# Windowed attention of a hybrid backbone: one pass over the scores, with the exponentials transposed on TensorE

## The chip, the cores and the metric

The kernel runs on one core of one Trainium2 chip. The metric is the device time of one execution in microseconds (us). A core has a matrix engine (TensorE, PE in the profile, with its weight loads as PEld), a vector engine (VectorE, DVE), an activation engine (ScalarE, ACT), a general engine (GpSimd, POOL) and a queue for transfers (SyncE, SP). Each runs its own instructions in a fixed order and waits for the others by semaphores.

## What is computed

Two layers of a transformer-like backbone over 256 context tokens and 1024 latent tokens of width 1024. In each layer one input projection feeds three mixers, whose outputs are concatenated and go through one output projection; a gated MLP follows. The change concerns the third mixer, attention in a window, with 8 query heads of width 64 in two groups of four that share keys and values:

```
s_loc = einsum(q, kw) * scale          # keys of the query's block of 128 and of both neighbours
s_loc = where(|kpos - qpos| <= 128, s_loc, NEG_INF)
s_ctx = einsum(q, kc) * scale          # all 256 context keys
p = softmax(concat([sink, s_ctx, s_loc], -1))
o = p[ctx] @ vc + p[loc] @ vw
```

Context queries attend to the 256 context keys alone, and only in layer 0. Everything is float32; the kernel reaches that precision on TensorE by splitting values into a high and a low part of type fp32r and adding the products.

## The kernel before

Tokens are in 10 blocks of 128, blocks 0 and 1 being context. `gq_units` (L1446) makes one unit for each block of queries and each group of heads: 20 units in layer 0 (4 of them context, with 2 blocks of keys) and 16 in layer 1. A latent unit has 5 blocks of keys, 2 of context and 3 local ones, or 4 at the ends of the sequence; the two layers have 84 and 76 pairs of unit and key block. A unit has two parts, each a generator.

`scores` (L1477) only finds row maxima. Queries are on the partitions of the output: for each of four heads a product of the high parts over 128 rows (L1498) and one of the leftovers over 64 rows (L1499), over 256 context columns and over up to 384 local ones, each into a bank of PSUM named `gs`. VectorE reduces them (L1505 for context, L1512 for local, which also adds the band mask), takes the minimum with the sink (L1516, L1518), and `max_rows` (L1214) turns the four columns of maxima into rows of the query tile by a product with the identity (L1223, into `mT`).

`values` (L1522) computes the scores again, this time with keys on partitions and the four heads' queries in 512 columns, with the maxima now subtracted by the product itself: for each block of keys a mask product where needed (L1544), the high product (L1546) and the leftovers and maxima (L1547), into a `gs` bank. ScalarE takes the exponential into `gx` (L1550), VectorE rounds it to `gp`'s high part (L241), GpSimd subtracts for the low part (L245), and three products with V follow (L1555 to L1557, into `o`), delayed by up to four blocks (`GDL`). V has a column of ones, so that row 64 of `o` is the sum of the exponentials. `unflip` (L1228) copies `o` and transposes it back (L1235, into `yT`).

What sets the order: `streams` walks over the units' two parts by their costs, with up to `GQL` units of lead for `scores`, and a scheduler then places each engine's instructions, the unit before (`df_units`, the second mixer) having the higher priority (`HPO`). So the windowed attention begins while the second mixer ends. In that mixer, score products over 512 columns go to `ds` (L1376, L1363), ScalarE takes exponentials in place (L1356), later products go to `ds` again (L1419), ScalarE takes exponentials (L1420) and the product with V is L1432; L1412 transposes its result by a product with `fold`.

The banks are what the two share least: `df_p` holds three (two `ds`, one `od`), and the windowed attention has these:

```
p_b = self.psum(f"pb{l}", {n: ("b", 4) for n in (None, "gs", "mT", "yT")})
p_o = self.psum(f"po{l}", {"o": ("o", 1)} if ODB + XB == 3 else {})
```

So `gs`, `mT` and `yT` take turns in four banks, and the result has one. The band mask `band3` has a place of its own in both layers. The output projection of the first blocks (L249 to L251, into `op`; its transposes L1630) is already woven into the end of the windowed attention.

## Time and profile before

| | us |
|---|---|
| median of 3 runs | 4549.56 |
| lowest and highest | 4540.59, 4586.83 |
| the profiled execution | 4560.47 |
| span of the profiled execution | 4558.6 |
| PE busy | 4169.8 (91%) |
| PEld busy | 3182.7 (70%) |
| DVE busy | 2917.1 (64%) |
| ACT busy | 1797.8 (39%) |
| POOL busy | 2180.7 (48%) |

The span runs from the first to the last instruction. Matmuls are pipelined, so that the record of one begins before that of the one ahead has ended: what a product costs in a stream is the distance from its start to the next start, not its length. A product of plain float32 data has two records. The granted clock of TensorE has two levels, 2.4 GHz (1.00 in the views) and 1.2 GHz (0.50), and a stretch's figure is the mean; over the span it is 0.892.

### The profile page before, as it was taken

The numbers are of one execution on the slowest core, as the hardware profiler recorded it, in microseconds if no ns is written. First come the engines' busy times: TensorE is split into PE (matmuls) and PEld (weight loads), VectorE is DVE, ScalarE is ACT, GpSimd is POOL, SyncE is SP. The second block draws the span as 40 slices with busy tenths as digits, with TensorE's granted clock in tenths as the row PEclk, the third lists the DMA queues.
The fourth block names the chain that finished last, engine by engine and source line by source line (L and its number), as shares of the span: only waits on it lengthen the run. The fifth ranks groups of instructions, "written<-read, shape, count | busy, mean of one in ns | idle before, by whom it ended". The sixth has DMA issues, their size and how long they took to land.

```text
span 4558.6 us, 67583 instructions
## 1 busy us (share of the span) xinstructions
PE 4169.8 (91%) x24447; PEld 3182.7 (70%) x24447; DVE 2917.1 (64%) x5849; ACT 1797.8 (39%) x3586; POOL 2180.7 (48%) x2151
## 2 busy tenths in 40 slices
PE   8998888898998799979998998888989998999898
PEld 5886655665466699968996786645845466788786
DVE  4346676567665877788777336766677656766443
ACT  3334554544323333343333334555534333333332
POOL 3335324334353666666665425264243445766443
PEclk9997778796899899989998998668988988999999
DMA  6454232234023222232223646132241142222443
GB/s 205 137 135 109 62 85 78 69 95 119 27 68 126 93 84 78 81 116 88 79 84 114 166 115 144 43 80 60 59 121 34 29 133 87 79 83 84 146 149 121
DMA packets 465626, 440.44 MB, mean 97 GB/s; under 512 B 122115, under 2 KB 389515, under 8 KB 465292
## 3 DMA queue, kind: packets, MB, share of 16 engines
q1 hardware_dynamic: 408780, 369.39, 27.4%
q0 software_dynamic: 24352, 62.80, 4.9%
q10 hardware_dynamic: 32160, 3.94, 0.5%
q8 instruction: 193, 3.16, 0.3%
q14 instruction: 141, 1.16, 0.1%
HBM read 340.96 MB, written 95.04 MB: 96 GB/s over the span
## 4 chain that ended last, share of the span: by engine, by line
PE 73%; DVE 13%; DMA 5%; ACT 3%; issue 3%; POOL 2%; SPq 1%; ACTq 0%; DVEq 0%; POOLq 0%
PE m L249 6%; PE m L250 6%; PE m L251 6%; PE b L249 3%; PE b L250 3%; PE od L1432 3%; PE b L251 3%; PE gs L1499 2%; PE gram L955 2%; PE dn L249 2%; PE dn L250 2%; PE dn L251 2%; PE ds L1419 2%; PE gs L1498 2%; PE fm L249 2%
## 5 line engine op out<-in xcount | busy, mean ns | idle before, releaser
L245 POOL TENSOR_TENSOR gp<-gx,gp 128x512 fp32r<-128x512 f32 x160 | 208.4, 1307 | 257.3 <-DVE gp L241 181.9
L239 ACT ACTIVATE fwh<-wraw 128x1024 fp32r<-128x1024 f32 x198 | 206.0, 1055 | 273.0 <-DVE wraw L1849 190.8
L1356 ACT ACTIVATE ds<-ds,dnm 128x512 f32<-128x512 f32 (+1 forms) x400 | 232.4, 581 | 189.2 <-DVE dnm L1378 112.4
L1420 ACT ACTIVATE p<-ds 128x512 f32<-128x512 f32 (+1 forms) x336 | 187.2, 585 | 254.8 <-PE ds L1419 211.8
L245 DVE TENSOR_TENSOR wl<-wraw,fwh 128x1024 fp32r<-128x1024 f32 x110 | 196.8, 1790 | 114.0 <-ACT fwh L239 111.8
L245 POOL TENSOR_TENSOR wl<-wraw,fwh 128x1024 fp32r<-128x1024 f32 x88 | 222.4, 2530 | 95.8 <-ACT fwh L239 95.5
L249 PE MATMUL m<-h,fwh 128*128 128x322 f32 (+1 forms) x660 | 219.8, 333 | 11.0 <-ACT fu L1895 6.8
L1378 DVE TENSOR_REDUCE dnm<-ds 128x1 f32<-128x512 f32 x256 | 173.6, 686 | 84.9 <-PE ds L1376 82.2
L251 PE MATMUL m<-h,wl 128*128 128x322 f32 (+1 forms) x660 | 218.8, 332 | 2.9 <-DVE wl L245 2.9
L245 DVE TENSOR_TENSOR wl<-wr,wh 128x512 fp32r<-128x512 f32 (+1 forms) x76 | 66.6, 878 | 241.8 <-ACT wh L239 128.2
L250 PE MATMUL m<-h,fwh 128*128 128x322 f32 (+1 forms) x660 | 220.1, 334 | 0.0
L245 POOL TENSOR_TENSOR wl<-wr,wh 128x512 fp32r<-128x512 f32 (+1 forms) x76 | 99.8, 1313 | 246.8 <-ACT wh L239 208.1
L1425 DVE SCALAR_TENSOR_TENSOR p<-p,ls 128x512 f32<-128x512 f32 (+1 forms) x168 | 144.8, 863 | 95.3 <-ACT p L1420 93.3
L1432 PE MATMUL od<-p,vh 128*64 128x512 f32 (+1 forms) x336 | 191.0, 707 | 13.4 <-DVE p L1425 9.2
L1376 PE MATMUL ds<-ks,qs 96*128 96x512 f32 x256 | 155.5, 625 | 44.5 <-ACT ds L1356 37.5
L250 PE MATMUL dn<-dl,ahl 128*128 128x512 f32 x440 | 177.5, 403 | 4.4 <-POOL dl L245 4.4
L249 PE MATMUL dn<-dh,ahl 128*128 128x512 f32 x440 | 175.3, 402 | 5.2 <-ACT ahl L239 3.8
L245 POOL TENSOR_TENSOR dl<-dr,dh 128x1024 fp32r<-128x1024 f32 x44 | 109.5, 2489 | 143.2 <-ACT dh L239 143.2
L249 PE MATMUL m<-T,fwh 128*128 128x322 f32 (+1 forms) x436 | 147.1, 338 | 32.7 <-DVE fraw L1866 23.7
L251 PE MATMUL dn<-dh,ahl 128*128 128x512 f32 x440 | 171.4, 399 | 0.0
L1419 PE MATMUL ds<-qs,ks 104*128 104x512 f32 (+1 forms) x336 | 152.7, 496 | 8.8 <-ACT p L1420 5.9
L245 DVE TENSOR_TENSOR dd<-dr,dd 128x1024 fp32r<-128x1024 f32 x44 | 59.0, 1344 | 156.9 <-ACT dd L239 156.9
(572 smaller groups left out, 13490.3 us busy)
## 6 DMA issues: line engine op xcount, KB each, us to landing
dr<-in_ff_w_down_dram SPq DMA_DIRECT2D x88, 512.0 KB
aw<-in_ada_w_dram SPq DMA_DIRECT2D x160, 256.0 KB
wraw<-in_ff_w_gate_dram SPq DMA_DIRECT2D x66, 512.0 KB
wraw<-in_ff_w_up_dram SPq DMA_DIRECT2D x66, 512.0 KB
wr<-in_w_in_dram SPq DMA_DIRECT2D x88, 256.0 KB
x<-scr_x SPq DMA_DIRECT2D x28, 512.0 KB
scr_act<-cv POOLq DMA_DIRECT2D x22, 512.0 KB, 3.0
ar<-scr_act SPq DMA_DIRECT2D x44, 256.0 KB
```

Of the source, the lines that this page charges most:

```text
L239: nc.scalar.activation(hi, src, AF.Copy)
L245: e.tensor_tensor(out=lo, in0=src, in1=hi, op=ALU.subtract)
L249: mm(out, lh, rh, start=first, stop=False)
L250: mm(out, lh, rl, start=False, stop=False)
L251: mm(out, ll, rh, start=False, stop=last)
L1356: act.activation(s, s, AF.Exp, bias=nm[:, c, m, i:i + 1], accum_out=L[:, c, m, i:i + 1])
L1376: mm(s, us["q"][m][0:96, i * 128:i * 128 + 128], K2[m][0:96, 256 + 512 * c:768 + 512 * c], start=True, stop=True)
L1378: vv.tensor_reduce(out=nm[:, 1 + c, m, i:i + 1], in_=s, axis=AX.X, op=ALU.max, negate=True)
L1419: mm(s[:, :w], hs["K"][m][0:104, j * 128:j * 128 + 128], us["q"][m][0:104, :w], start=True, stop=True)
L1420: act.activation(p[:, m, :w], s[:, :w], AF.Exp)
L1425: vv.scalar_tensor_tensor(out=p[:, 0, :w], in0=p[:, 1, :w], scalar=self.nlam, in1=p[:, 0, :w], op0=ALU.mult, op1=ALU.add)
L1432: mm(o[r:r + 64, :w], v[:, j], p[:, 0, :w], start=j < 2, stop=j >= nk - 2)
```

## The change

Each unit now makes one pass. `scores` takes the heads in pairs, (0, 2) and (1, 3). A pair's local scores go to two `gs` banks and its context scores to a third. VectorE finds the maxima as before, and ScalarE then takes the exponentials from the same banks, with queries on partitions, the maximum as a bias and the sum as an accumulated output (L1542, L1544 of the new kernel), into a tile `ge` for each head. `max_rows`, the mask product and the column of ones are gone. `values` transposes the exponentials, four heads to a `gs` bank (L1571), ScalarE copies the bank to the high part (L1573), VectorE subtracts for the low part from PSUM (L1574), and two products follow: the high part with [V high, V low] side by side in 128 columns (L1580), and the low part with V high (L1581). The result's two halves are added by a float32 product with `gfold` (L1563). The leftovers of heads 2 and 3 lie on partitions 64 to 127 of the query and key tiles, so that a pair's leftover products use different row halves (L1508; the high products are L1504). Leads and delays become 1, `gp` has three buffers, and a unit's second pair is not begun before the unit ahead has issued its transposes. The costs that `streams` uses change. In layer 0 `band3` takes a buffer of the tag `cv`, and it is loaded by SP's queue where it was GpSimd's.

```diff
-GQL = (2, 2)
+GQL = (1, 1)
...
-GPB = 4
+GPB = 3
...
-GXB = 2
-GDL = (4, 4)
-GHI = "v"
-GLO = "p"
+GDL = (1, 1)
...
     def gq_consts(self):
-        self.mask8 = self.mask("mask8", 64)
-        self.identr = self.al("identr", [128, 128], 1, F32R)
-        self.nc.vector.tensor_copy(self.identr, self.ident)
+        self.gfold = self.al("gfold", [128, 64])
+        for i in range(2):
+            self.nc.gpsimd.tensor_copy(self.gfold[64 * i:64 * i + 64], self.ident[64 * i:64 * i + 64, 64 * i:64 * i + 64])
         self.band3 = None
...
+                            self.cast(k[0:64], self.scr_gk[g, 128:192, tok])
+                            self.cast(k[64:128], self.scr_gk[g, 128:192, tok])
...
+                v = [self.al(t, [128, n, 128], b, F32R, "gv") for t, n, b in (("hA0", 5, 8), ("fB", 4, 8), ("gv", 1, 2))]
...
-            us = {}
+            us = {"before": prev[0]}
+            prev[0] = us
...
-                    self.band3 = self.al("band3", [128, 384], 1, F32R)
-                    self.cast(self.band3, self.a["k_band"])
+                    self.band3 = self.al("band3", [128, 384]) if l == DEPTH - 1 else self.al("cv", [128, 384], 2, n="band3")
+                    self.load(self.band3, self.a["k_band"])
...
+                self.cast(q2[64:128, 256:512].rearrange("p (h t) -> p h t", h=2), src[0:64, 2:4])
...
+                for hp in ((0, 2), (1, 3)):
+                    if hp[0] and us["before"]:
+                        while not us["before"].get("done"):
+                            yield 0.3
+                    n2 = slice(hp[0], 4, 2)
+                    sl = []
+                    if nloc:
+                        sl = [self.bk("gs") for _ in hp]
+                        for k, c, x in pieces(kts[2], nloc):
+                            for s, h in zip(sl, hp):
+                                main(s[:, x], h, k, c)
+                            for s, h in zip(sl, hp):
+                                rest(s[:, x], h, k, c, h // 2)
                         b = (kts[2] - qt + 1) * 128
...
+                        for s, h in zip(sl, hp):
+                            vv.tensor_tensor_reduce(out=s[:, :nloc * 128], in0=s[:, :nloc * 128], in1=self.band3[:, b:b + nloc * 128],
+                                                    scale=-GQ_SCALE, scalar=3.0e38, op0=ALU.add, op1=ALU.min, accum_out=m2[:, 1, h:h + 1])
+                    sc = self.bk("gs")
+                    for i, h in enumerate(hp):
+                        x = slice(256 * i, 256 * i + 256)
+                        main(sc[:, x], h, 0, slice(0, 256))
+                        rest(sc[:, x], h, 0, slice(0, 256))
+                    vv.tensor_reduce(out=m2[:, 0, n2], in_=sc.rearrange("p (i k) -> p i k", i=2), axis=AX.X, op=ALU.max, negate=True)
...
+                    yield 1.2
+                    for i, h in enumerate(hp):
+                        P = us["P"][h] = self.al("fraw", [128, 640], 2, n="ge") if h == 3 else self.al("ge", [128, 640], 5)
+                        if nloc:
+                            act.activation(P[:, 256:256 + nloc * 128], sl[i][:, :nloc * 128], AF.Exp, bias=nm[:, h:h + 1], scale=-1.0,
+                                           accum_out=L[:, 1, h:h + 1])
+                        act.activation(P[:, 0:256], sc[:, 256 * i:256 * i + 256], AF.Exp, bias=nm[:, h:h + 1], scale=GQ_SCALE,
+                                       accum_out=L[:, 0, h:h + 1])
+                    yield 1.2
...
-                    u = self.unflip(o, 4, 65, "xj")
...
+                    act.activation(s, o, AF.Copy)
+                    u = self.bk("yT")
+                    for h in range(4):
+                        mm(u[:, h * 64:h * 64 + 64], s[:, h * 128:h * 128 + 128], self.gfold, start=True, stop=True)
...
                 for i, kt in enumerate(kts):
-                    s = self.bk("gs")
...
-                    mm(s, KH[kt // 6][:, c], q1, start=not mask, stop=False)
-                    mm(s, KL[kt // 6][0:72, c], q2[0:72], start=False, stop=True)
-                    x = self.al("gx", [128, 512], GXB)
+                    t = self.bk("gs")
+                    for h in range(4):
+                        nc.tensor.transpose(t[:, h * 128:h * 128 + 128], us["P"][h][:, i * 128:i * 128 + 128], self.ident)
                     p = self.al("gp", [128, 2, 512], GPB, F32R)
-                    act.activation(x, s, AF.Exp, scale=GQ_SCALE)
-                    self.split(p[:, 1], p[:, 0], x, GHI, GLO)
+                    act.activation(p[:, 1], t, AF.Copy)
+                    vv.tensor_tensor(out=p[:, 0], in0=t, in1=p[:, 1], op=ALU.subtract)
+                    if i == n - 1:
+                        us["done"] = True
...
-                        mm(o[0:65], v[:, 0:65], p[:, 1], start=i == 0, stop=False)
-                        mm(o[0:64], v[:, 65:129], p[:, 1], start=False, stop=False)
-                        mm(o[0:65], v[:, 0:65], p[:, 0], start=False, stop=i == len(kts) - 1)
+                        high = lambda: mm(o, v, p[:, 1], start=i == 0, stop=i == n - 1)
+                        low = lambda: mm(o[0:64], v[:, 0:64], p[:, 0], start=False, stop=False)
+                        for f in (low, high) if i else (high, low):
+                            f()
...
-            units.append((scores, values, 3.3, 6.5, 0))
+            units.append((scores, values, 5.0 if len(kts) > 2 else 3.0, 1.4 * len(kts), 0))
```

Two places where instructions stand otherwise. The first is the transfer of the band mask in layer 0, without which no local unit can be reduced. On GpSimd's queue in the kernel before it stands among the loads of the first queries and the values' low parts:

```order
L1470 MEMSET gv_11306 128x1
L1470 MEMSET gv_11354 128x1
L1208 DMA band_11509<-in_k_band_dram 128x384
L245 TENSOR_TENSOR gv_11306<-gvr_11302,gv_11306 128x64
L245 TENSOR_TENSOR gv_11354<-gvr_11350,gv_11354 128x64
```

On SP's queue in the changed kernel (`dsq` are the second mixer's results, the last of them of its last unit; `y` is the first tile of the output projection):

```order
L207 DMA scr_y<-dsq_11004 128x2x64
L207 DMA scr_y<-dsq_11128 128x4x64
L207 DMA scr_y<-dsq_11235 128x4x64
L207 DMA dng_27050<-in_df_norm_g_dram 128x64
L207 DMA band_11567<-in_k_band_dram 128x384
L207 DMA y_13614<-scr_y 128x1024
```

The load has moved from the start of the windowed attention to behind the last result of the second mixer.

The second place is PE's order in layer 0 in the stretch after the second mixer. Before (`op` is the output projection, `yTo` its transposes):

```order
L1630 MATMUL yTo_13682<-ident,y_13676 128x128 x4
L250 MATMUL op_13663<-ow_13421,yh_13576 128x512
L251 MATMUL op_13663<-ow_13421,yl_13577 128x512
L249 MATMUL op_13663<-ow_13426,yh_13576 128x512
L1498 MATMUL gs_12807<-kg_11341,gq_12752 128x384
L1499 MATMUL gs_12807<-kg_11345,gq_12752 128x384
L1498 MATMUL gs_12811<-kg_11341,gq_12752 128x384
L1499 MATMUL gs_12811<-kg_11345,gq_12752 128x384
L1546 MATMUL gs_12815<-gq_12638,kg_11293 128x512
L1547 MATMUL gs_12815<-gq_12638,kg_11297 128x512
```

Now, in the same stretch, the last transposes of one unit and the first scores of the next:

```order
L1571 MATMUL gs_11783<-ident,ge_11711 128x128
L1571 MATMUL gs_11783<-ident,ge_11733 128x128
L1580 MATMUL o_11736<-gp_11742,gv_11353 128x512
L1581 MATMUL o_11736<-gp_11742,gv_11353 64x512
L1504 MATMUL gs_11800<-kg_11291,gq_11793 128x384
L1508 MATMUL gs_11800<-kg_11295,gq_11793 128x384
L1581 MATMUL o_11736<-gp_11768,gv_11353 64x512
L1580 MATMUL o_11736<-gp_11768,gv_11353 128x512
L1504 MATMUL gs_11801<-kg_11291,gq_11793 128x384
L1508 MATMUL gs_11801<-kg_11295,gq_11793 128x384
```

The second score products and the projection between them are gone from here, a unit's scores now stand behind the transposes of the unit ahead, and a high product is followed by its own leftover product, not by that of the other head of the pair.

## Rows read from the trace of the kernel before

**Rows 1.** Windows: length, busy PE, PEld, DVE, ACT, POOL (count); clock, DMA, GB/s

```profile
1046.00:1275.00 229.00, 217.18 (x808) 120.39 (x808) 159.18 (x411) 87.33 (x202) 89.09 (x93) 0.80 0.19 55
1275.00:1375.00 100.00, 97.38 (x404) 59.59 (x405) 60.84 (x173) 27.57 (x55) 52.82 (x62) 1.00 0.23 75
3400.00:3650.00 250.00, 236.50 (x900) 131.13 (x901) 172.34 (x456) 97.84 (x230) 98.03 (x99) 0.85 0.13 36
3650.00:3707.00 57.00, 53.05 (x212) 32.10 (x210) 35.97 (x86) 20.50 (x39) 31.19 (x24) 0.91 0.34 111
```

**Rows 2.** Groups by form, PE, 1275 to 1375: busy us, mean ns, idle before

```profile
L1557 PE MATMUL o<-gp,gv 128*65 128x512 f32 x37 | 15.2, 410 | 1.3 <-POOL gp L245 1.3
...
L250 PE MATMUL op<-ow,yh 128*128 128x512 f32 x12 | 4.8, 401 | 0.0
...
L1630 PE MATMUL yTo<-ident,y 128*128 128x128 f32 x20 | 3.1, 275 | 0.0
```

**Rows 3.** Timeline of PE at clock 1.00: start, length, what

```profile
1259.61 0.40 PE L1547 MATMUL gs<-gq,kg 72*128 72x512 f32 x1
1259.84 1.00 PE L1412 MATMUL ds<-fold,doT 128*128 128x64 f32 x8
1260.65 0.31 PE L1498 MATMUL gs<-kg,gq 128*128 128x128 f32 x1
...
1261.15 0.38 PE L1498 MATMUL gs<-kg,gq 128*128 128x256 f32 x1
...
1261.77 0.33 PE L1498 MATMUL gs<-kg,gq 128*128 128x128 f32 x1
...
1303.19 0.34 PE L1498 MATMUL gs<-kg,gq 128*128 128x384 f32 x1
...
1303.83 0.50 PE L251 MATMUL op<-oh,yl 128*128 128x512 f32 x1
...
1306.72 0.60 PE L1630 MATMUL yTo<-ident,y 128*128 128x128 f32 x4
...
1307.39 0.39 PE L251 MATMUL op<-ow,yl 128*128 128x512 f32 x1
```

**Rows 4.** Windows, the product with V (L1555) alone: PE busy, PEld busy; clock, DMA

```profile
1046.00:1275.00 229.00, 21.30 (x46) 7.45 (x46) 0.80 0.19 55
...
3400.00:3650.00 250.00, 25.24 (x57) 8.63 (x57) 0.85 0.13 36
```

**Rows 5.** Windows, the second mixer's product with V alone, layer 0

```profile
750.00:800.00 50.00, 24.11 (x36) 4.03 (x36) 0.81 0.33 94
```

**Rows 6.** Timeline of PE: score products of the second mixer, 1029 to 1033

```profile
1029.43 0.79 PE L1376 MATMUL ds<-ks,qs 96*128 96x512 f32 x1 [0.70 <-ACT ds L1356]
...
1032.31 0.80 PE L1376 MATMUL ds<-ks,qs 96*128 96x512 f32 x1 [0.78 <-ACT ds L1356]
```

**Rows 7.** Groups by form, DVE, 1275 to 1375

```profile
L1512 DVE CUSTOM_DVE_ANT_0 gs<-gs,band 128x384 f32<-128x384 f32 x19 | 10.7, 565 | 9.5 <-PE gs L1499 9.2
L1505 DVE TENSOR_REDUCE gmx<-gs 128x2 f32<-128x512 f32 x12 | 8.3, 692 | 7.3 <-PE gs L1499 7.2
...
L1512 DVE DVE_READ_ACCUMULATOR2_ANT gmx<- 128x1 f32 x27 | 3.8, 141 | 0.0
...
L1633 DVE TENSOR_TENSOR yl<-yTo,yh 128x512 fp32r<-128x512 f32 x4 | 2.7, 687 | 0.7 <-ACT yh L1632 0.7
```

**Rows 8.** Timeline of ACT: exponentials with a sum, one behind the other

```profile
1057.13 0.44 ACT L1356 ACTIVATE ds<-ds,dnm 128x256 f32<-128x256 f32 x1
...
1057.72 0.45 ACT L1356 ACTIVATE ds<-ds,dnm 128x256 f32<-128x256 f32 x1
```

**Rows 9.** Groups by form, ACT, 1275 to 1375

```profile
L1550 ACT ACTIVATE gx<-gs 128x512 f32<-128x512 f32 x36 | 20.6, 594 | 35.3 <-PE gs L1547 23.7 <-POOL gp L245 10.5 <-PE gs L1499 1.2
```

**Rows 10.** Windows in which PE is often idle, columns as in rows 1

```profile
600.00:650.00 50.00, 36.31 (x208) 17.83 (x209) 41.12 (x138) 23.23 (x60) 11.85 (x15) 0.64 0.35 83
800.00:850.00 50.00, 36.06 (x288) 25.30 (x288) 28.29 (x77) 25.09 (x75) 18.23 (x39) 0.53 0.31 76
```

More of the change, by code (lines that the diff above doesn't have):

```diff
@@ L423, in at_params @@
         self.nsink = self.sm([128, 8], "nsink", 1)
-        nc.vector.tensor_scalar(out=self.nsink, in0=self.sink, scalar1=-1.0 / GQ_SCALE, scalar2=None, op0=ALU.mult)
+        nc.vector.tensor_scalar(out=self.nsink, in0=self.sink, scalar1=-1.0, scalar2=None, op0=ALU.mult)
         lv = self.al("lv", [128, 4, 32])
@@ L1501, in scores @@
-                for h in range(0, 4, 2):
-                    s = self.bk("gs")
-                    for i in range(2):
-                        prod(s[:, i * 256:i * 256 + 256], h + i, 0, 2)
-                    vv.tensor_reduce(out=m2[:, 0, h:h + 2], in_=s.rearrange("p (i k) -> p i k", i=2), axis=AX.X, op=ALU.max, negate=True)
-                    yield 0.5
-                if nloc:
-                    for h in range(4):
-                        s = self.bk("gs")
-                        prod(s[:, :nloc * 128], h, kts[2], nloc)
-                        b = (kts[2] - qt + 1) * 128
-                        vv.tensor_tensor_reduce(out=s[:, :nloc * 128], in0=s[:, :nloc * 128], in1=self.band3[:, b:b + nloc * 128], scale=-1.0, scalar=3.0e38,
-                                                op0=ALU.add, op1=ALU.min, accum_out=m2[:, 1, h:h + 1])
-                        yield 0.5
@@ L1515, in scores, with main @@
[L1515 to L1520 removed]
+                            yield i0 // 6, slice((i0 % 6) * 128, (i0 % 6 + i1 - i0) * 128), slice((i0 - k0) * 128, (i1 - k0) * 128)
+                def main(o, h, k, c):
+                    mm(o, q1[:, hc(h)], KH[k][:, c], start=True, stop=False)
@@ L1522, in values @@
             def values(g=g, qt=qt, kts=kts, us=us, hs=hs):
-                KH, KL = hs["K"]
-                q1, q2 = us["q1"], us["q2"]
                 o = self.bk("o")
+                n = len(kts)
                 def result():
                     es = self.al("ges", [128, 4], 2)
-                    vv.scalar_tensor_tensor(out=es, in0=us["nm"], scalar=GQ_SCALE, in1=self.sink[:, 4 * g:4 * g + 4], op0=ALU.mult, op1=ALU.add)
+                    gp.tensor_tensor(out=es, in0=us["nm"], in1=self.sink[:, 4 * g:4 * g + 4], op=ALU.add)
@@ L1530, in result @@
                     act.activation(es, es, AF.Exp)
-                    u = self.unflip(o, 4, 65, "xj")
-                    vv.tensor_tensor(out=es, in0=u[:, :, 64], in1=es, op=ALU.add)
+                    for i in range(2 if n > 2 else 1):
+                        gp.tensor_tensor(out=es, in0=us["L"][:, i], in1=es, op=ALU.add)
                     vv.reciprocal(out=es, in_=es)
+                    s = self.al("xj", [128, 512], 1, n="oT")
+                    act.activation(s, o, AF.Copy)
+                    u = self.bk("yT")
@@ L1538, in values @@
                 for i, kt in enumerate(kts):
-                    s = self.bk("gs")
-                    c = slice(kt % 6 * 128, kt % 6 * 128 + 128)
-                    mask = kt >= 2 and kt != qt
-                    if mask:
-                        b = (qt - kt + 1) * 128
-                        mm(s.rearrange("p (h t) -> p h t", h=4), self.identr,
-                           self.band3[:, b:b + 128].unsqueeze(1).broadcast_to([128, 4, 128]), start=True, stop=False)
-                    mm(s, KH[kt // 6][:, c], q1, start=not mask, stop=False)
```

43 lines of the change are left out of this document (21 added, 22 removed).

## The prediction, made blind

> **What bounds the kernel now.** I read the windows first, over the two stretches in which the windowed attention runs: 1046 to 1375 us in layer 0 and 3400 to 3707 in layer 1 [rows 1]. In all four PE is busy for 93 to 97% of the time, DVE for 61 to 70%, the others less. The first window of each layer is shared with the end of the second mixer, at a clock of 0.80 and 0.85; from 1275 on the windowed attention is alone, but for some output projection, at 1.00. Busy PE says little where records overlap, so the timeline comes next [rows 3]: starts follow each other without a hole, a 512-column product each 0.23 us, though its record is 0.40 long. PE's stream is the bound, then, and its price list is: 0.23 for 512 columns; 0.62 and 0.64 for a high product and its leftover over 256 and 384 columns (the change to 64 rows and back is in it); 0.44 for four transposes (0.67 from 1306.72 to 1307.39, less one product); 0.81 for the float32 product that folds a result. Third, the groups give the pace of the stretch alone [rows 2]: 37 blocks of keys in 100 us, or 7.4 units of five, beside 36 projection products (8.3) and 20 transposes (2.2). That is 89.5 / 7.4 = 12.1 us for a unit. The list gives nearly that: 27 wide products 6.2, eight pairs 5.0, four transposes for the way back 0.44, and some 0.2 for the maxima (a quarter of the fold): 11.9.
>
> **PE's share of the change.** A unit of five blocks now has eight pairs as before (5.0), 20 transposes (2.2), ten wide products (2.3) and the fold (0.81): 10.3, or 1.6 less. Over the 160 blocks and 36 units, 856 wide products (five a block and 56 masks) and the 0.64 a unit go, 220 us; 160 x 0.44, 320 x 0.23 and 36 x 0.81 come, 173 us. PE alone gains 47 us, and 54 at the clock of 0.86 that the four windows have on average.
>
> The leftovers in row halves add nothing to this: by the order of instructions a high product is followed by its own leftover, and only 5 of 304 leftovers stand directly behind another. The Trainium skill says (TensorEngine Tiling (Array Packing), Key Properties) that different tiles of the array can load and multiply at the same time. Two leftovers side by side would save one switch, some 0.27 us, for each of 64 pairs of local heads: 17 us; in the order as it stands, 1 us. No row of this trace shows two halves at work, and the sum takes nothing for it.
>
> **The others' share.** Per unit ScalarE made five exponentials of 0.59 [rows 9] and two small steps, 3.7 us. Now it makes eight with a sum and five copies. A 256-wide one with its sum takes 0.59 from start to start [rows 8]; a 384-wide one lies between that and half as much again, 0.64 taken, because the width costs only a part. So 4 x 1.23 + 5 x 0.6 + 0.8 (the result's copy and the sink) = 8.7. VectorE keeps four local reductions of 0.71 (0.565 + 0.141) and two of 0.69, loses the casts and the mask of maxima, and gets five subtractions from PSUM at 0.69, the row of the same operation in the projection [rows 7]: about 8.9 where it was 8.4. GpSimd loses 160 subtractions and gets a third query load a unit; it is the bound nowhere. All three lie under PE's 10.3, so on sums alone the gain would stand.
>
> **Banks.** But the four banks that were held for one short step each are now held across three engines. Before, a bank waited for a pair of products and a reduction, or for two products and an exponential: some 1.8 us, 13 times a unit, 6 us of four banks. Now a local bank is held from its product through its reduction, the context scores of the pair (2 x 0.62), their reduction, the minima and up to four exponentials. I go through one unit as the order has it after the second mixer: transposes, next unit's first pair, second pair, transposes. Two prices are estimates: 0.1 for a handover, between nothing and the 0.15 from the end of one exponential's record to the start of the next [rows 8], and 0.3 for the minima, twice the 0.141 of VectorE's smallest step [rows 7].
>
> - from the first four transposes to a free bank for the next scores: 0.44, a copy 0.60, three subtractions 2.07, handovers 0.3: 3.4;
> - first pair: two local pairs 1.28, context 1.24, products with V between them 0.92, reduction 0.69, minima 0.3, four exponentials 2.46, handovers 0.4: 7.3;
> - second pair: its local scores fit beside the first's exponentials, but its context bank comes only with the third of them, so behind the last remain 0.74 of products, 0.69, 0.3, 2.46 and handovers 0.2: 4.4.
>
> That is 15.1 us a unit where PE needs 10.3 and where it was 12.1. From below it is bounded by the banks' time without any gap: a pair alone takes 6.4, of which its local banks are held for 4.6 and 5.2 and the context bank for 5.1; with five transposes of 2.0 and 1.5 for the way back that is 41 bank-us, on four banks 10.3, no more than PE's own part. From above by the same chain with PE's part (4.2: transposes 0.44, four products of a pair's scores, 2.52, the last 0.74 and half of V's) at the lower clock, 19.3. I take 15.1, since the order shows just this succession. The Trainium skill (TensorEngine Tiling (Array Packing), PSUM Bottleneck) has the general case: a faster TensorE does not empty PSUM any faster, and the copies may become the bound. The trace of before does not show it, there PE is the bound; by PE's list alone the sum would be -47, by the banks it is what follows.
>
> **Layer 0.** Its mask is loaded behind the second mixer's last result (the first piece of the order), and the reductions of every local unit wait for it, with four banks full; so all 76 local blocks run behind the mixer, where in the order of before 43 of 84 blocks do. The end of the mixer with the four context units takes 229 us less the local work done in it, 38 of the 46 blocks [rows 4] at 12.1 a five, 92: 137. From below: 22 blocks of its second part at 50 / 18 = 2.78 (two records each, [rows 5]), 61; 25 score steps at 1.44 [rows 6], 36; four context units of 5.4 (ten wide products, four pairs, 0.64): 119. Taken: 128. Then 15.2 fives x 15.1 = 230, and 3 for projection products that stood here. 361 against 329: +32.
>
> **Layer 1.** The mask is loaded early, and mixing stays: by the order 40 blocks run beside the mixer (53 before), 36 alone (23 before). The shared window loses 17 of its 57 blocks [rows 4], 3.4 fives x 12.1 / 0.85 = 48, and PE's 1.6 / 0.85 on eight fives, 15: 250 - 63 = 187 (202 if stalls eat the second). Alone 7.2 x 15.1 = 109, and 11 of projection that moves behind it. 307 against 307: 0.
>
> **Sum.** +32 us on the profiled 4560.47, which lies 10.9 above the median of the runs; on the median 4549.56 + 32 = 4582. In one line, with u for the pace: change = 22.4 u - 306. It is nothing at 13.7, +45 at 15.7 and -45 at 11.7. (One per cent, 45 us, is about what a measurement of this kernel tells from no change.)
>
> **Rivals.**
> - *PE stays the bound.* The scheduler may have packed pairs and transposes closer than my chain, and the shared window hides more. For it: PE's busy share of 93 to 97% before, and that 10.3 us of bank time would allow it. Against: it needs four banks without a gap, and one unit's chain leaves them idle for a third. It gives -47 to -54: 4495 to 4503.
> - *The clock falls (slower).* At 15.1, PE works 10.3, 68%. The windows with PE busy for 72% have a clock of 0.64 and 0.53 [rows 10], the stretch alone had 1.00. At 0.6 the 4.2 us of PE on the chain become 7: u = 17.9, +95, or 4645. It decides from u = 15.7, that is when the chain's PE part grows by 0.6. Against: the shared windows had 0.80 and 0.85 and PE's work was dense enough.
> - *The mask arrives earlier than I think*, and layer 0 mixes like layer 1: then u counts for half as many units in layer 0, about -10: 4540. Against it: the order.
>
> **How the numbers follow.** Forecast, banks at a pace of 12 to 15.7: 0.45, and alone it spans 4515 to 4595. Clock or further stalls: 0.36. PE stays the bound: 0.15. Early mask: 0.04. Within 1% lie 0.43 of the forecast's chance and the early mask's 0.04; the forecast's fastest 0.02 and the PE case are just past it on one side, the second rival on the other. So faster by over 1% 0.17, the same 0.47, slower 0.36. The range begins at 4503, which leaves part of the PE case out, and ends at 4655, past the clock's 4645.
>
> **What would show it.** In the changed trace: after the mixer of layer 0, units 14 to 16 us apart, PE idle for some 30% and waiting for DVE's subtractions (L1574) and ACT's exponentials (L1542, L1544); no local reduction (L1526) in layer 0 before the last L1429; clock under 1.00 in the stretch alone; layer 1's shared part shorter, its part alone longer. Units 12 us apart or less with PE dense would prove the banks wrong; a clock near 0.6 there the second rival right.

## The result, and the profile after

The changed kernel takes 4718.11 us, the median of 4 runs (4699.56 to 4727.83); the kernel before took 4545.52 beside it. The ratio is 1.0355 (95% interval 1.0318 to 1.0391): slower by 3.6%, and 63 us past the end of the range. The profiled execution took 4699.56, its span is 4697.7 and its mean granted clock 0.864, where before had 4558.6 and 0.892.

These are the windows of the changed kernel over the windowed attention of layer 0 (the end of the second mixer, then behind it) and of layer 1 (shared, then alone). The columns are those of [rows 1].

```profile
1046.00:1175.00 129.00, 97.42 (x388) 49.44 (x388) 73.00 (x195) 68.20 (x182) 24.68 (x46) 0.67 0.26 81
1175.00:1465.00 290.00, 255.01 (x927) 176.75 (x927) 123.67 (x329) 118.78 (x360) 32.62 (x105) 0.71 0.13 36
3490.00:3725.00 235.00, 204.84 (x786) 126.25 (x787) 127.37 (x358) 123.32 (x363) 32.84 (x80) 0.70 0.14 37
3725.00:3850.00 125.00, 108.75 (x396) 74.50 (x397) 57.31 (x145) 58.66 (x168) 21.19 (x41) 0.69 0.26 82
```

Layer 0 ends at 1465 where it ended at 1375. The mixer's end with the first local scores took 129 us where 128 were forecast. The agreement is in part luck: the mixer's last products end at 1158, and then PE stands idle for 12.8 us until the first tile of the output projection has come, a start that no term of the forecast had.

```profile
1171.18 1.08 PE L1656 MATMUL yTo<-ident,y 128*128 128x128 f32 x4 [12.84 <-DMA y<-scr_y]
```

Behind it 76 local blocks took 290 us, 15.2 fives of 19.1 us, not of 15.1. The clock stood at 0.80 to 1.00 in [rows 1] and stands at 0.67 to 0.71 in all four windows now. PE is busy for 88% of the second window, which sounds like a full engine; but its products are longer at the lower level. So the waits come next: who waited for whom, from 1175 to 1465 (us in total, times, longest).

```profile
POOL gq L1205 <- PE gs L1508: 191.2, 13, 19.2
ACT gp L1573 <- PE gs L1571: 79.4, 37, 7.4
ACT oT L1560 <- PE o L1580: 62.0, 16, 6.8
DVE gs L1526 <- PE gs L1508: 45.2, 32, 3.4
...
DVE gp L1574 <- ACT gp L1573: 28.2, 27, 1.8
...
PE yT L1563 <- ACT ge L1542: 17.6, 14, 1.6
...
PE gs L1504 <- ACT ge L1542: 7.7, 9, 1.2
```

PE itself waits little, mostly once a unit, some 1.3 us, ahead of the fold for the last head's exponentials. The other engines wait much more, and for PE. That is a slow PE, and the groups of the same stretch show that no other engine's step was sized too low (busy us, mean ns of one, idle before): the copy takes 0.60, the subtraction 0.69 and the local reduction 0.565 us, as in [rows 7, 9]. Four exponentials with their sums take 2.0 us (1392.28 to 1394.30), less than the 2.46 in the forecast.

```profile
L1571 PE MATMUL gs<-ident,ge 128*128 128x128 f32 x304 | 70.7, 391 | 4.9 <-ACT ge L1542 4.6 <-DVE gy L1565 0.3
```

```profile
L1573 ACT ACTIVATE gp<-gs 128x512 fp32r<-128x512 f32 x76 | 44.0, 599 | 85.2 <-PE gs L1571 79.4 <-PE o L1581 4.4 <-PE o L1580 1.1
```

```profile
L1574 DVE TENSOR_TENSOR gp<-gs,gp 128x512 fp32r<-128x512 f32 x76 | 50.5, 685 | 28.6 <-ACT gp L1573 28.2
L1526 DVE CUSTOM_DVE_ANT_0 gs<-gs,band 128x384 f32<-128x384 f32 x48 | 27.1, 565 | 45.9 <-PE gs L1508 38.3 <-ACT gp L1573 2.7 <-ACT ge L1544 2.4
```

The clock's course behind the mixer is the main thing to see. These windows of the changed kernel are cut where the granted clock steps (columns as above): the longest piece at the lower level, one unit inside it, and six steps near the end.

```profile
1273.90:1342.20 68.30, 63.07 (x179) 42.85 (x179) 23.07 (x61) 22.72 (x72) 6.78 (x18) 0.50 0.12 34
1281.40:1304.90 23.50, 21.84 (x62) 14.84 (x62) 8.16 (x21) 7.55 (x24) 2.58 (x8) 0.50 0.19 57
...
1386.50:1396.80 10.30, 9.42 (x29) 6.40 (x28) 4.25 (x11) 4.40 (x13) 0.32 (x2) 0.50 0.04 13
1396.80:1403.60 6.80, 5.44 (x26) 3.39 (x25) 3.49 (x10) 3.04 (x11) 1.86 (x4) 1.00 0.24 64
1403.60:1413.80 10.20, 9.04 (x27) 5.90 (x26) 4.50 (x12) 3.92 (x14) 0.40 (x2) 0.50 0.06 18
1413.80:1420.70 6.90, 5.65 (x23) 3.22 (x21) 3.59 (x11) 2.82 (x8) 0.20 (x1) 0.99 0.00 0
1420.70:1430.90 10.20, 9.19 (x34) 7.29 (x34) 3.86 (x10) 4.96 (x17) 0.40 (x2) 0.50 0.04 13
1430.90:1437.70 6.80, 5.66 (x23) 3.29 (x21) 3.69 (x12) 2.48 (x8) 0.67 (x7) 1.00 0.00 0
```

Near the end the clock goes to and fro: 10.2 us at 1.2 GHz with PE busy for some 90%, then 6.8 at 2.4 GHz with PE busy for 80 to 83%, 17 us a turn, about as long as one of the shorter units. There PE waits for the unit's chain at the upper level, and the clock falls; at the lower level PE is denser, and the clock comes back. That is not the whole course. From 1273.9 to 1342.2 the clock stayed at 1.2 GHz for 68 us although PE was busy for 92%, and two units inside it took 23.5 us each; what brings the clock back is not shown. From fold to fold a unit of five blocks takes 15.7 to 23.5 us in this stretch, and in a second execution (r1) the same units take the same time within 0.2 us, but for one (20.0 for 23.4). PE's timeline inside one turn gives its prices at both levels (start, length, what).

```profile
1386.79 0.67 PE L1504 MATMUL gs<-kg,gq 128*128 128x384 f32 x1
1387.39 0.69 PE L1508 MATMUL gs<-kg,gq 64*128 64x384 f32 x1
1388.01 0.58 PE L1504 MATMUL gs<-kg,gq 128*128 128x256 f32 x1
1388.52 0.58 PE L1508 MATMUL gs<-kg,gq 64*128 64x256 f32 x1
1389.03 0.58 PE L1504 MATMUL gs<-kg,gq 128*128 128x256 f32 x1
...
1390.05 0.79 PE L1580 MATMUL o<-gp,gv 128*128 128x512 f32 x1
1390.64 1.05 PE L1571 MATMUL gs<-ident,ge 128*128 128x128 f32 x4
1391.35 0.78 PE L1581 MATMUL o<-gp,gv 128*64 128x512 f32 x1
...
1394.35 0.63 PE L1580 MATMUL o<-gp,gv 128*128 128x512 f32 x1
1394.77 1.91 PE L1571 MATMUL gs<-ident,ge 128*128 128x128 f32 x8
...
1399.09 0.28 PE L1504 MATMUL gs<-kg,gq 128*128 128x256 f32 x1
1399.30 0.38 PE L1508 MATMUL gs<-kg,gq 64*128 64x256 f32 x1
1399.62 0.39 PE L1504 MATMUL gs<-kg,gq 128*128 128x256 f32 x1
...
1402.28 1.10 PE L1563 MATMUL yT<-gfold,oT 128*128 128x64 f32 x8 [1.25 <-ACT ge L1542]
1403.23 0.39 PE L1571 MATMUL gs<-ident,ge 128*128 128x128 f32 x2
```

From start to start a pair costs 1.22 over 384 columns and 1.02 over 256 at the lower level, and 0.53 over 256 at the upper one; at the lower level four transposes cost 0.71 (their record is 1.05 long), and a 512-column product 0.42 to 0.59, about twice the 0.23 of [rows 3]. A unit's list at the lower level is 4 x 1.22 + 4 x 1.02 + 5 x 0.71 + 10 x 0.5 + 1.9 for the fold (twice its 0.95) = 19 us, an estimate from these rows. Where a unit's local keys lie in two pieces (products over 256 and 128 columns in place of 384) the list is longer: the unit from 1281.4 to 1304.9, at the lower level from end to end, has PE busy for 21.84 of 23.5 us. So at 1.2 GHz PE is nearly the bound by itself, while at 2.4 GHz it waits for the chain.

Where the 139 us of the two profiles arose is read by stage, from the first score step of a layer's second mixer, the first product with V of the windowed attention, and the last one (columns of the table below):

| kernel | median | span | layer 0: mixer and windowed | layer 1: mixer ahead | layer 1: windowed |
|---|---|---|---|---|---|
| before | 4549.56 | 4558.6 | 945 | 554 | 292 |
| changed | 4718.11 | 4697.7 | 1033 | 589 | 332 |
| once more (r1) | 4717.99 | 4716.2 | 1031 | 599 | 335 |
| early mask (a1) | 4614.91 | 4633.0 | 1005 | 550 | 314 |
| products for transposes (a2) | 4728.93 | 4729.3 | 1052 | 598 | 325 |
| two more banks (a3) | 4691.01 | 4692.4 | 1001 | 923 with the next | |
| one filler a unit (a4) | 4658.32 | 4650.5 | 1019 | 558 | 313 |
| 16 fillers a unit (a5) | 4656.76 | 4668.5 | 1026 | 560 | 325 |
| before, late mask (b1) | 4630.68 | 4620.9 | 999 | 590 | 288 |
| no low part (d1) | 4619.77 | 4627.6 | 993 | 593 | 281 |
| early mask, more banks late (c1) | 4600.60 | 4635.1 | 967 | 595 | 311 |
| c1 with 7 fillers (c5) | 4637.22 | 4648.3 | 954 | 608 | 319 |
| c1, V two blocks behind (c6) | 4606.46 | 4602.5 | 959 | 588 | 286 |
| c1, scores two ahead (c7) | 4614.09 | 4608.7 | 949 | 599 | 299 |
| c6 and c7 (e1) | 4608.84 | 4594.3 | 950 | 575 | 296 |
| c6, banks from the fifth tile (e2) | 4597.30 | 4569.5 | 955 | 570 | 288 |

Layer 0 has +88, the windowed attention of layer 1 +40, the mixer ahead of it +35 and all the rest -24. Each row of stages is one execution, and it need not be the median one: the profiled executions of a1, a5, c1 and c5 lie 13 to 37 us above their medians, those of the changed kernel, e1 and e2 13 to 26 below. The changed kernel and r1 are one program, and their stages differ by up to 10 us.

### The profile page after: what moved, and what is told of

Read it like the earlier page. It is cut to its first block, busy times and chain, and to the rows that moved or that the text cites. A ratio compares the mean times of both kernels' runs of the same rounds, so it can differ in the third digit from the quotient of the medians.

```text
span 4697.7 us, 68383 instructions
## 1 busy us (share of the span) xinstructions
PE 4235.1 (90%) x24623; PEld 3269.4 (70%) x24623; DVE 2876.8 (61%) x5735; ACT 1933.5 (41%) x4130; POOL 2017.8 (43%) x2121
## 4 chain that ended last, share of the span: by engine, by line
PE 71%; DVE 12%; DMA 6%; ACT 4%; issue 3%; POOL 3%; SPq 1%; ACTq 0%; POOLq 0%; DVEq 0%
PE m L246 5%; PE m L247 5%; PE m L248 5%; PE od L1429 3%; PE b L246 3%; PE b L248 3%; PE b L247 3%; PE gs L1571 3%; PE gs L1508 2%; PE ds L1416 2%; PE dn L246 2%; PE dn L247 2%; PE dn L248 2%; PE gs L1504 2%; PE gram L952 2%
## 5 line engine op out<-in xcount | busy, mean ns | idle before, releaser
L1205 POOL DMA_DIRECT2D gq<-scr_gq x108 | 58.9, 556 | 354.7 <-PE gs L1508 348.6
L1571 PE MATMUL gs<-ident,ge 128*128 128x128 f32 x640 | 148.4, 384 | 11.1 <-ACT ge L1542 5.5
```

The source lines that it names most:

```text
L1571: nc.tensor.transpose(t[:, h * 128:h * 128 + 128], us["P"][h][:, i * 128:i * 128 + 128], self.ident)
```

## The experiments

**Is it the late mask?** a1 gives the mask a buffer that is free early; b1 gives the old design the late one.

```diff
-... else self.al("cv", [128, 384], 2, n="band3")
+... else self.al("fB", [128, 512], 8, n="band3")[:, :384]
```

> The changed kernel with one edit: in layer 0 the mask takes a buffer of a tag that is free early, so the local blocks run beside the second mixer again. Late-mask theory (the loss of layer 0, 90 us, is mostly lost mixing): the time falls by 40 to 90 us, to 4628 to 4678, and the local reductions of layer 0 begin well before 1174 us. Pace theory (a unit of five costs about 19 us because TensorE stands at its lower level, wherever the unit runs): the local work moves, but the windows with it keep a granted clock near 0.7 and the time stays within 25 us of 4718.

4614.91 us, 1.0112 of before (1.0060 to 1.0164): 103 less, more than either theory had. The first local reduction of layer 0 now starts at 1119.5, well ahead of the mixer's last product at 1225.4. Between the profiles, layer 0 gives back 28 us and layer 1's windowed attention 18; the largest piece is 39 in layer 1's mixer, of which more below, and 20 are lost in the rest. So of the 88 us of layer 0 the early mask takes back a third.

```diff
-self.band3 = self.al("band3", [128, 384], 1, F32R)
+self.band3 = self.al("band3", [128, 384], 1, F32R) if l == DEPTH - 1 else self.al("cv", [128, 384], 2, F32R, "band3")
```

> The kernel before with one edit: in layer 0 the mask takes the buffer that the changed kernel gives it, which is free only behind the second mixer, so all 76 local blocks of layer 0 run behind the mixer, with the old way of doing them. Theory that the late mask costs little and the new pace is what costs: the mixer's end takes about 128 us, then 15.2 fives of 12.1 follow, 312 against 304, so the time is that of before within 25 us. Theory that lost mixing is a cost of its own: 4590 or more.

4630.68, 1.0169 (1.0131 to 1.0207): the second theory. The windows behind the mixer, of all work and (in the second fence) of the last product with V alone, one a block:

```profile
1170.00:1200.00 30.00, 13.88 (x43) 8.52 (x42) 12.32 (x44) 3.67 (x7) 5.04 (x7) 0.56 0.26 87
1200.00:1430.00 230.00, 223.87 (x806) 132.76 (x804) 135.56 (x357) 53.69 (x105) 111.27 (x118) 0.87 0.14 41
```

```profile
1170.00:1200.00 30.00, 0.00 (x0) 0.00 (x0) 0.56 0.26 87
```

The local units start from nothing: for 30 us not one block is finished and PE is busy for less than half of the time, while the first scores, maxima and exponentials go through. After that PE is dense, at a clock of 0.87 where [rows 1] had 1.00. Layer 0 is 54 us longer for the late mask alone, in a design whose pace was not changed. The working in the expectation had 312 against 304 there. Another 36 us of b1's loss stand in layer 1's mixer, where nothing was edited.

**Do the transposes hold the clock down?** a2 makes them ordinary float32 products with the identity.

```diff
-nc.tensor.transpose(t[:, h * 128:h * 128 + 128], us["P"][h][:, i * 128:i * 128 + 128], self.ident)
+mm(t[:, h * 128:h * 128 + 128], us["P"][h][:, i * 128:i * 128 + 128], self.ident, start=True, stop=True)
```

> The changed kernel with its 640 forward transposes written as ordinary float32 products with the identity, everything else as it is. Theory that the transposes themselves hold the clock down: the granted clock of the stretch behind the mixer of layer 0 rises from 0.71 to over 0.9 and the time falls by 40 us or more in all. Theory of gaps (TensorE waits for exponentials and banks, and the clock falls for that): the clock stays between 0.6 and 0.8; the time goes by what an ordinary product costs beside a transpose, within plus or minus 30 us of 4718.

4728.93, 1.0382 (1.0324 to 1.0440): the theory of gaps. Behind the mixer the clock is 0.77 with more records of PE, and the blocks come no faster, 49 in the 200 us from 1200 where the changed kernel has 52. The transposes are not what makes the kernel slow; whether they count for less with the clock than products do is not shown, since the products in their place also give PE more to do.

**Banks.** a3 puts the transposed exponentials into the mixer's two score banks.

```diff
-                    t = self.bk("gs")
+                    t = self.bk("ds")
```

> The changed kernel with the transposed exponentials in the two PSUM banks of the second mixer's scores, so that the four banks of the scores are no longer shared with them. Bank theory: the waits of the query loads and of the scores for a bank shrink, the unit behind the mixer of layer 0 falls from 19.1 us to 12 to 16, and the time falls by 50 to 120 us. Theory that the exponentials of the last head (TensorE's wait of 17.6 us in all ahead of the fold) and the clock set the pace, not the banks: the unit stays at 17 to 20 and the time within 25 us of 4718.

4691.01, 1.0283 (1.0241 to 1.0324), between the two. The pace behind the mixer rises to 59 blocks in 200 us, 16.9 us a five, and layer 0 ends 32 us earlier; but the mixer holds these banks until its end, so in layer 1 the transposes of all units moved behind it, and nothing was won there. c1 therefore takes the two banks only for units that run behind the mixer, and has the early mask.

```diff
-                    t = self.bk("gs")
+                    t = self.bk("ds" if qt >= (5, 7)[l] else "gs")
```

> The changed kernel with the early mask of layer 0, and with the transposed exponentials in the second mixer's two score banks for the units that run behind the mixer (from the sixth query tile in layer 0, the eighth in layer 1). If mask and banks are separate costs, the gains add up: 4615 less some 20 to 40, 4575 to 4600. If the clock takes back what the banks give, it stays at 4600 to 4635.

4600.60, 1.0112 (1.0066 to 1.0158): on the line between the two outcomes, and by the ratio no better than a1. By stage the gains add up in layer 0, which takes 967 where a1 took 1005, while layer 1's mixer takes 595 where a1 had 550.

**Gaps and the clock.** a4 adds one product a unit in layer 0 where PE waits for the last head; a5 adds sixteen; c5 adds seven to c1.

```diff
+                if l == 0 and qt >= NCTX:
+                    mm(self.bk("od"), self.ident, us["P"][1][:, 0:512], start=True, stop=True)
```

> The changed kernel with one more 512-column product per unit in layer 0, whose result nothing reads, issued before the transposes of the unit. It adds work to TensorE: 28 products of 0.23 us at the upper level, some 7 us, 14 at the lower. Theory of gaps (the clock falls because TensorE waits): the wait ahead of the fold is filled, the granted clock of 1175 to 1465 rises above 0.80, and the time is 4718 or less in spite of the added work. Theory that the number of handovers alone sets the pace, or that the transposes hold the clock: the clock stays near 0.71 and the time is 4718 to 4732.

4658.32, 1.0213 (1.0171 to 1.0254). (There are 16 of these products, not 28.) The clock behind the mixer rises to 0.78, short of the 0.80 expected, and layer 0 is 14 us shorter in spite of the added work. But most of the 60 us came in layer 1, where nothing was edited: 31 in the mixer and 19 in the windowed attention.

```diff
+                    if l == 0 and nloc:
+                        us["q"] = q1
+                        for _ in range(3):
+                            mm(self.bk("od"), q1[:, 0:128], KH[0][:, 0:512], start=True, stop=True)
                     yield 1.2
...
+                    if l == 0 and qt >= NCTX:
+                        for _ in range(2):
+                            mm(self.bk("od"), us["q"][:, 0:128], hs["K"][0][0][:, 0:512], start=True, stop=True)
                     t = self.bk("gs")
```

> The changed kernel with 16 more 512-column products in each unit of layer 0 that has local blocks (three behind each pair's scores, two ahead of each four transposes; nothing reads them), some 245 in all: 3.7 us of TensorE a unit at the upper level, which brings the unit to 14 us of TensorE where the chain over the banks is 15.1. Theory that the clock falls for want of work on TensorE: the granted clock behind the mixer of layer 0 rises from 0.70 to 0.9 or more, the stretch behind the mixer falls from 305 us to 220 to 270, although 57 us of work at full clock are added. Theory that the clock is not set by the gaps: the clock stays at 0.70 to 0.80 and the stretch grows to 350 or more.

4656.76, 1.0220 (1.0162 to 1.0278). One window behind the mixer, columns as above:

```profile
1175.00:1457.00 282.00, 275.83 (x1125) 178.48 (x1125) 123.19 (x324) 117.74 (x360) 31.46 (x104) 0.91 0.14 37
```

With PE busy for 98% the clock is 0.91: the clock did fall for want of work. But the stretch is 282 us where it was 290, neither of the two outcomes. One reason is the price of a filler product: at the clock of 1.00 it takes 0.34 us from its start to that of the next other instruction, and 0.55 to that of a second filler, where the expectation had 0.23. So filler holds the clock up and takes the time that the clock gives back.

c5 has one in each of the two places, in the units of either layer that use the two more banks.

> The kernel with the early mask and the two more banks, and in its units behind the mixer of either layer seven more 512-column products (one behind each pair's scores, one ahead of each four transposes; nothing reads them), 1.6 us of TensorE a unit at the upper level. Theory that what is left of the loss is the clock, which falls in TensorE's waits: the granted clock behind the mixer rises from 0.77 to over 0.85 and the time falls below 4600, to 4550 to 4590. Theory that added work costs what it takes: 16 units by 1.6 to 3.5 us, 4625 to 4655.

4637.22, 1.0154 (1.0108 to 1.0199): slower than c1 by 37, as the second theory has it. The two profiled executions are only 13 apart, so the stages do not account for all of it: in layer 0, at a clock of 0.85, 13 us are won, and in layer 1 the mixer and the windowed attention lose 13 and 8.

**Is it a chain?** d1 leaves out the subtraction and the product with it (the low part of the exponentials), in the changed kernel with its late mask and four banks.

```diff
-                    vv.tensor_tensor(out=p[:, 0], in0=t, in1=p[:, 1], op=ALU.subtract)
...
-                        for f in (low, high) if i else (high, low):
-                            f()
+                        high()
```

> The changed kernel without the low part of the exponentials: the 160 subtractions from PSUM and the 160 products with them are left out, so the result has only the high part of the exponentials in it. Theory that the unit's chain over the three engines sets the pace, and the clock follows from it: three of the five subtractions lie on the chain (2.1 us of a unit) and five products of 0.23 to 0.5 go from TensorE, so the unit behind the mixer of layer 0 falls from 19 us to 15 to 17.5 and the time by 40 to 80 us, while the clock stays between 0.6 and 0.8. Theory that TensorE alone sets the pace, at whatever clock it has: only the products go, 1.2 to 2.4 us a unit, 15 to 30 us in all.

4619.77, 1.0119 (1.0068 to 1.0170), 98 less in the medians and 70 between the profiled executions. The pace went from 52 to 59 blocks in 200 us, 19.2 to 16.9 us a five, at a clock of 0.66. Layer 0 wins 40, layer 1's windowed attention 51. This does not decide between the theories. In the changed kernel the product with the low part costs PE 0.28 us at the upper level and 0.53 at the lower (means from start to start in the stretch), so five a unit are 1.4 to 2.6 us, and the pace gained 2.3. All 160 of them are 45 to 85 us; the 15 to 30 of the expectation counted only some 12 of the 36 units. A unit of d1 at the lower level from end to end waits as little outside PE as the one of the changed kernel above, 1.6 us against 1.7:

```profile
1319.70:1338.70 19.00, 17.43 (x50) 11.37 (x50) 4.98 (x16) 7.53 (x24) 2.25 (x7) 0.50 0.12 33
```

So it is a3 that shows the chain over the banks: it takes little off PE (see the last section) and won the same 2.3 us a five.

**Leads.** c6 and c7 change one line each of c1; e1 has both lines, e2 is c6 with `(4, 7)` in place of `(5, 7)`.

```diff
-GDL = (1, 1)
+GDL = (2, 2)
```

```diff
-GQL = (1, 1)
+GQL = (2, 2)
```

> The kernel with the early mask and the two more banks, and the products with V two blocks behind their transposes instead of one. Theory that TensorE's waits for the subtraction (8 us of its 13 behind the mixer of layer 0) start the drops of the clock: the time falls by 10 to 40 us from 4600. Theory that the later products only move the wait to the transposes: within 15 us of 4600.

> The kernel with the early mask and the two more banks, and the scores of a unit let two units ahead of its products instead of one. Theory that the chain from the scores to the exponentials is what TensorE waits for: the time falls by 10 to 40 us from 4600. Theory that the buffers of the exponentials (a second pair waits for the transposes of the unit before) hold the order as it is: within 10 us of 4600.

4606.46 (1.0094, 1.0052 to 1.0137) and 4614.09 (1.0108, 1.0078 to 1.0139): by the totals no gain. By stage there is one: layer 0 takes 959 and 949 us, layer 1's windowed attention 286 and 299, where before had 945 and 292. Once mask, banks and leads are mended, these two stages together are within some 10 us of the old ones (1245 and 1248 against 1237, one profile each). Most of what is left stands in layer 1's mixer, 588 and 599 against 554.

c6 also shows what PE's stream by itself allows. From 1329.0 to 1376.7 its clock stays at 1.00, and three units there follow each other in 11.4 to 11.9 us with PE busy for 97%:

```profile
1331.90:1366.90 35.00, 33.78 (x164) 21.57 (x163) 22.00 (x64) 22.20 (x69) 3.90 (x18) 1.00 0.09 25
```

There the banks hardly hold PE up, and PE is the bound again. But the unit takes 11.4 or more, not the 10.3 of the forecast's list, against 12.1 before: even with PE full, one pass gains little.

**The mixer that nobody edited.** r1 is the changed kernel again, without an edit.

> The changed kernel once more, unaltered, for a second profile. The part of the second mixer of layer 1 that runs before any windowed attention took 589 us in its first profile, 554 in the kernel before, 550 and 558 in the kernels with the early mask and with the filler, though its instructions are the same in all. If the clock's course in it belongs to the program, it is 580 to 600 again; if it is chance from one execution to the next, it can be anything from 545 to 600.

599 us, so most of it belongs to the program. Here are the windows of this stage, in before, in the changed kernel and in a4:

```profile
2860.00:3415.00 555.00, 496.00 (x4294) 329.56 (x4293) 380.43 (x887) 286.97 (x703) 232.49 (x375) 0.79 0.29 72
```

```profile
2920.00:3509.00 589.00, 521.31 (x4286) 346.48 (x4284) 383.81 (x885) 291.21 (x713) 233.64 (x373) 0.75 0.27 69
```

```profile
2922.00:3481.00 559.00, 495.60 (x4287) 331.37 (x4286) 382.11 (x882) 289.88 (x713) 232.61 (x369) 0.79 0.30 72
```

The work is the same and the clock is not: 0.79 x 555 = 438, 0.75 x 589 = 442, 0.79 x 559 = 442. The scheduler places the rows of this stage in another order after an edit elsewhere; kernels with nearly the same order there mostly agree (changed, r1 and a2: 589, 599, 598; c1 and c7: 595, 599; before and a1: 554, 550). But c6 and e1 have nearly the same order too, and took 588 and 575, so the order does not settle it alone. One place that differs is the start of the fourth head, whose keys arrive late: PE's wait there in the changed kernel, and in a4, which has other products to do meanwhile.

```profile
PE ds L1360 <- DMA ks<-scr_df: 7.0, 1, 7.0
```

```profile
PE ds L1360 <- DMA ks<-scr_df: 2.9, 1, 2.9
```

> The kernel with the early mask and the two more banks (from the sixth query tile in layer 0, the eighth in layer 1), products with V two blocks behind and scores two units ahead. In the kernels so far the part of layer 1's second mixer ahead of any windowed attention took 588 to 599 us in six that start its fourth head with only two products of other work in the 25 rows before, 550 to 560 in four that have 15 to 22 there and 593 and 608 in two others that have 15; here it is 10. Theory that the order of that unchanged part is what still separates the mended kernel from the one before: if it takes 550 to 575 here, the time is 4550 to 4580; if 588 to 608, 4590 to 4625. Theory that the windowed attention itself is still slower: over 4590 with a short mixer as well.

> The same with the two more banks from the fifth query tile in layer 0 and scores one unit ahead; the order of layer 1's second mixer is of the same kind as in the run with both leads at two. By the theory of its order the same two outcomes as there, 4550 to 4585 with a mixer of 550 to 575, 4590 to 4625 with one of 588 to 608; its windowed attention should take as long as with later products alone, 300 to 330 us in layer 0 from its first product and 280 to 295 in layer 1.

The mixer took 575 and 570, and the times are 4608.84 (1.0093, 1.0065 to 1.0121) and 4597.30 (1.0070, 1.0042 to 1.0098), over the 4580 and 4585 that the theory of the order had for a short mixer. By its expectation e1 falls to the theory that the windowed attention itself is still slower; its profile has +5 in layer 0 and +4 in layer 1's windowed attention, which is little. e2's profiled execution has a span of 4569.5 with layer 0 at 955 and layer 1's windowed attention at 288, but its ten runs go from 4571 to 4612. So the order of the mixer may be part of what is left, but that is not shown, and what else differs from execution to execution stays open. No version here beats the kernel before.

## Why the prediction was wrong

- **The place and the kind were right.** No local reduction of layer 0 starts before 1169.8, behind the mixer's last product; leftovers stand apart and gain nothing; copies, subtractions and reductions have the lengths taken. Too few banks hold the pace down (a3), and the late mask costs layer 0 time (a1, b1). That the mixer's end took 129 us (128 taken) is in part luck, since 12.8 of them are a wait that was in no term.
- **The step that failed is the pace, "That is 15.1 us a unit", with the clock left at 1.00.** Measured were 19.1. The rival of the falling clock, given 0.36, was what happened: 0.71 in the stretch. It was sized too low as well: I let the lower level stretch the chain's 4.2 us of PE to 7, which made 17.9. But at the lower level PE's whole list, some 19 us and up to 21.84, is longer than the chain, and PE becomes nearly the bound there. Whether the changed kernel would keep 15.1 at a clock of 1.00 no run shows. 15.2 x 4.0 = 61 more than forecast; layer 0 came to +88 where +32 + 61 = +93.
- **"PE's work was dense enough" failed for the same reason.** I took the shared windows' clock from before. With PE waiting in every unit the clock did not stay there; a5 shows that it goes with the work.
- **PE's own list was too short.** 10.3 us a unit were taken, 1.6 less than before; with PE full at the clock of 1.00, c6's units take 11.4 to 11.9. So the rival in which PE stays the bound would have gained far less than its 47 us.
- **Layer 1, "307 against 307: 0", has +40.** Its shared part was forecast with the clock of 0.85, 187 us. From 15 us ahead of its first product (as in before) to 3725 it took 231; 187 x 0.85 / 0.70 is 227. The part alone, from there to the last product with V at 3841, took 116 where 120 were forecast. The same wrong clock again.
- **The late mask was priced as a loss of mixing only.** The forecast had local units at full pace from the first microsecond. b1 shows 54 us in the old design: a start of 30 us with no block finished, then a clock of 0.87 in place of 1.00.
- **+35 in layer 1's mixer was in no term.** The forecast took what lies outside the edited functions as fixed. It has the same work, in another order and at another clock; why the clock differs stays open.

## What to carry to other kernels

Where a chain leaves PE idle, price the stretch at both clock levels: PE's list at the lower one may be longer than the chain at the upper, and the stretch then pays for both in turn. An experiment that takes a step off a chain must be priced on every engine that the step used: d1 took a product off PE as well, and that alone can account for its gain. Work that is moved from beside another stage to behind it pays for its own start and for a colder clock even at an unchanged pace, so check when its first operand is loaded before rating its engines. Read experiments by stage: edits here moved an untouched stage by 35 to 45 us, as much as most of the effects that were looked for, and one program's stage moved by 10 us between two executions.

## What the runs showed of the hardware

Two leftovers in opposite row halves cost as much as one when they stand side by side. In a3, where more banks are free, 33 places of the order have leftovers next to each other (4 in the changed kernel). In 30 of them two leftovers of opposite halves start 3 to 7 ns apart; in the other three, where both are in one half, the starts are 0.22 to 0.38 us apart. A piece of PE's timeline there, at the clock of 1.00:

```profile
1163.93 0.38 PE L1508 MATMUL gs<-kg,gq 64*128 64x256 f32 x2
1164.24 0.38 PE L1504 MATMUL gs<-kg,gq 128*128 128x256 f32 x1
1164.56 0.38 PE L1508 MATMUL gs<-kg,gq 64*128 64x256 f32 x1
1164.87 0.39 PE L1504 MATMUL gs<-kg,gq 128*128 128x256 f32 x1
```

Both together last 0.38 us, and the next product starts 0.31 behind them, as it does behind the single one. The second leftover is free, and so is its switch. The Trainium skill (TensorEngine Tiling (Array Packing), Key Properties) says that different tiles load and multiply at the same time, and these rows agree. The Trainium skill (TensorEngine Tiling (Array Packing), Gotcha 1: PSUM Pressure) has different row tiles write to different PSUM banks; here that is so for the local scores of two heads, with a bank each, and not for the context scores, which share a bank and use one row half. So the leftovers come side by side only where both heads' banks are free at once: the shortage of banks that lengthened the chain also took away what the row halves were for.
